# Row normalization by the sum of absolute values: three buffers of 15 rows with the sums split over two engines, in place of four buffers of 13, 13, 13 and 12 rows

## The chip, the core and the metric

The kernel runs on one core of one Trainium2 chip. The metric is the device time of one execution in microseconds (us), the median of three runs. The other cores are idle. The data lies in the device's HBM, and the kernel brings it through the core's on-chip memory, whose 128 partitions are written `P`. It uses two compute engines, VectorE (DVE in the profile) and ScalarE (ACT), and two queues of transfers: the loads are issued by SyncE (SP), the stores by ScalarE.

## What is computed

```python
def setup_inputs():
    batch, seq, dim = 32, 512, 1024
    return {"x": np.random.randn(batch, seq, dim).astype(np.float32)}

def reference(x):
    sums = np.sum(np.abs(x), axis=-1, keepdims=True)
    return (x / (sums + 1e-8)).astype(np.float32)
```

There are 32 x 512 = 16384 rows of 1024 floats (4096 bytes). Each row is divided by the sum of its absolute values. Every element is read once and written once: 67.11 MB in, 67.11 MB out. Spread over 128 partitions, the work is 128 rows for each partition. In this text a "row" is such a row of all partitions together: 128 x 4096 bytes = 0.524 MB to load and as much to store.

## The kernel before

The 128 rows are cut into ten tiles of 13, 13, 13, 12, 13, 13, 13, 12, 13 and 13 rows. Four buffers, of 13, 13, 13 and 12 rows, are used in turn, so tile 4 takes the buffer of tile 0, and its load has to wait until the store of tile 0 has left that buffer.

```python
    R = 13
    SLOTS = [R, R, R, R - 1]
    # ... (cut: the list of the tiles' row counts)

    def piece(flat, i):
        a, k = P * sum(rows[:i]), rows[i]
        return flat[a : a + P * k, :].rearrange("(p r) d -> p r d", p=P)
```

A tile is one contiguous piece of HBM, and each partition gets a contiguous run of it: 13 rows are 13 x 4096 = 53248 bytes. Work on a tile of `k` rows, with `kv = k // 2`:

```python
        nc.vector.tensor_reduce(              # line 50: all k row sums, on VectorE
            out=s[:, :k], in_=x_tile[:, r0 : r0 + k, :],
            axis=mybir.AxisListType.X, op=mybir.AluOpType.add,
            apply_absolute_value=True,
        )
        nc.vector.tensor_scalar_add(out=s[:, :k], in0=s[:, :k], scalar1=EPS)    # line 57
        inv = stats.tile([P, R], FP32)
        nc.vector.reciprocal(out=inv[:, :k], in_=s[:, :k])                      # line 59
        nc.vector.tensor_mul(                 # line 60: scales the first kv rows in place
            out=x_tile[:, r0 : r0 + kv, :], in0=x_tile[:, r0 : r0 + kv, :],
            in1=inv[:, :kv].unsqueeze(2).to_broadcast([P, kv, d]),
        )
        for r in range(kv, k):                # line 67: ScalarE scales the others, row by row
            row = x_tile[:, r0 + r, :]
            nc.scalar.activation(out=row, in_=row,
                func=mybir.ActivationFunctionType.Copy, scale=inv[:, r : r + 1])
```

The loop over the tiles; each engine works through its own instructions in this order, and the engines wait for each other only where data asks for it:

```python
        for i, k in enumerate(rows):
            x_tile = slots[i % len(SLOTS)].tile([P, SLOTS[i % len(SLOTS)], d], FP32)
            nc.sync.dma_start(out=x_tile[:, :k, :], in_=piece(x_flat, i))       # line 77
            normalize(x_tile, 0, k, k // 2)
            nc.scalar.dma_start(out=piece(out_flat, i), in_=x_tile[:, :k, :])   # line 79
```

Of the kernel before, what the change touches and what calls it, by code (L numbers as in the profile page):

```python
# [1 line left out]

# [4 lines left out]

FP32 = mybir.dt.float32
EPS = 1e-8


@with_exitstack
def kernel(
    ctx: ExitStack,
    tc: tile.TileContext,
    x: bass.AP,
    out: bass.AP,
):
    nc = tc.nc
    P = nc.NUM_PARTITIONS  # L20

    x_flat = x.flatten_outer_dims()
    out_flat = out.flatten_outer_dims()
    n, d = x_flat.shape

    R = 13
    SLOTS = [R, R, R, R - 1]
    assert n % P == 0  # L30
    left = n // P
    rows = []
    while left:
        rows.append(min(left, SLOTS[len(rows) % len(SLOTS)]))
        left -= rows[-1]

    def piece(flat, i):
        a, k = P * sum(rows[:i]), rows[i]
        return flat[a : a + P * k, :].rearrange("(p r) d -> p r d", p=P)

    slots = [
        ctx.enter_context(tc.tile_pool(name=f"slot{b}", bufs=1))
        for b in range(len(SLOTS))
    ]
    stats = ctx.enter_context(tc.tile_pool(name="stats", bufs=4))

    def normalize(x_tile, r0, k, kv):

        s = stats.tile([P, R], FP32)
        nc.vector.tensor_reduce(  # L50
            out=s[:, :k],
            in_=x_tile[:, r0 : r0 + k, :],
            axis=mybir.AxisListType.X,
            op=mybir.AluOpType.add,
            apply_absolute_value=True,
        )
        nc.vector.tensor_scalar_add(out=s[:, :k], in0=s[:, :k], scalar1=EPS)  # L57
        inv = stats.tile([P, R], FP32)
        nc.vector.reciprocal(out=inv[:, :k], in_=s[:, :k])  # L59
        nc.vector.tensor_mul(  # L60
            out=x_tile[:, r0 : r0 + kv, :],
            in0=x_tile[:, r0 : r0 + kv, :],
            in1=inv[:, :kv].unsqueeze(2).to_broadcast([P, kv, d]),
        )
        for r in range(kv, k):
            row = x_tile[:, r0 + r, :]
            nc.scalar.activation(  # L67
                out=row,
                in_=row,
                func=mybir.ActivationFunctionType.Copy,  # L70
                scale=inv[:, r : r + 1],
            )

    with tc.manual_schedule():
        for i, k in enumerate(rows):
            x_tile = slots[i % len(SLOTS)].tile([P, SLOTS[i % len(SLOTS)], d], FP32)
            nc.sync.dma_start(out=x_tile[:, :k, :], in_=piece(x_flat, i))  # L77
            normalize(x_tile, 0, k, k // 2)
            nc.scalar.dma_start(out=piece(out_flat, i), in_=x_tile[:, :k, :])


# [1 line left out]
_INS = ['x']  # L83
_OUTS = [((32, 512, 1024), 'float32')]


# [23 lines left out]
```

## Time and profile before

| what | value |
|---|---|
| time, median of three runs | 317.93 us (317.73 to 318.16) |
| span of the profiled execution | 316.0 us |
| VectorE busy | 207.6 us, 66% of the span |
| ScalarE busy | 73.0 us, 23% of the span |
| bytes moved | 134.23 MB, mean 425 GB/s over the span |
| loads, 13 rows, from issue to landing (median) | 42.6 us |
| stores, 13 rows, from issue to landing (median) | 51.3 us |

A profile page describes one execution. It gives the busy time of each engine, then cuts the span into 40 slices of equal length (here 7.9 us) and shows for each, as a digit in tenths, how busy the engine was (9 is 90% or more). The row "DMA" does the same for the core's 16 transfer engines together, and the row "GB/s" says what they moved. "Landing" of a transfer is the moment at which those who wait for it learn that it is complete; "issue" is the moment at which the issuing engine hands it to its queue. The chain of waits starts from the last instruction and goes back, at each step, to what released it.

### The profile page before, as it was taken

How to read it: one execution, taken by the hardware profiler on the slowest of the kernel's cores; microseconds unless marked ns; L12 is line 12 of the kernel's file. 1: busy time of each engine (PE TensorE's matmuls, PEld its weight loads, DVE VectorE, ACT ScalarE, POOL GpSimd, SP SyncE). 2: the span in 40 equal slices, each digit the busy share in tenths (PEclk: the TensorE clock that was granted, in tenths of full speed). 3: DMA queues.
4: the chain of work that ended last, by engine and by line, in shares of the span. 5: the costliest groups of instructions: out<-in, count | busy, mean ns of one | idle time of the engine just before them, and what ended most of it. 6: DMA issues, size and time to landing. Idle time of an engine off the chain costs nothing.

```text
span 316.0 us, 219 instructions
## 1 busy us (share of the span) xinstructions
DVE 207.6 (66%) x40; ACT 73.0 (23%) x69; POOL 0.2 (0%) x4
## 2 busy tenths in 40 slices
DVE  0059999999479707980898099719941995299400
ACT  0010620803500700090009001800430036004500
POOL 0000000000000000000000000000000000000000
DMA  8999999999999999999999999999999999999995
GB/s 324 431 431 431 431 404 431 417 427 427 435 438 438 445 452 431 431 437 409 421 427 438 431 453 452 419 423 431 431 431 431 431 445 428 468 419 431 438 431 236
DMA packets 2881, 134.23 MB, mean 425 GB/s; under 512 B 320, under 2 KB 320, under 8 KB 320
## 3 DMA queue, kind: packets, MB, share of 16 engines
q1 hardware_dynamic: 1440, 67.11, 49.7%
q10 hardware_dynamic: 1440, 67.11, 49.0%
q14 instruction: 1, 0.01, 0.0%
HBM read 67.11 MB, written 67.11 MB: 425 GB/s over the span
## 4 chain that ended last, share of the span: by engine, by line
DVE 33%; DMA 33%; another core or an unknown queue 21%; ACT 6%; issue 0%; SPq 0%; DVEq 0%
DMA x_tile<-in_x_dram 33%; DVE s L50 26%; ACT x_tile L67 6%; DVE x_tile L60 6%; DVE inv L59 0%; DVE s L57 0%; SPq L77 0%; DVEq L59 0%
## 5 line engine op out<-in xcount | busy, mean ns | idle before, releaser
L50 DVE TENSOR_REDUCE s<-x_tile 128x13 f32<-128x13312 f32 (+1 forms) x10 | 138.1, 13806 | 86.6 <-DMA x_tile<-in_x_dram 86.6
L67 ACT ACTIVATE x_tile<-x_tile,inv 128x1024 f32<-128x1024 f32 x68 | 71.8, 1135 | 204.0 <-DVE inv L59 204.0
L60 DVE TENSOR_TENSOR x_tile<-x_tile,inv 128x6144 f32<-128x6144 f32 x10 | 65.6, 6558 | 0.3
L67 ACT ACT_TABLE_LOAD x1 | 1.3, 1283 | 19.5 <-DMA x_tile<-in_x_dram 19.5
L59 DVE RECIPROCAL inv<-s 128x13 f32<-128x13 f32 (+1 forms) x10 | 2.4, 238 | 0.8
L57 DVE TENSOR_SCALAR s<-s 128x13 f32<-128x13 f32 (+1 forms) x10 | 1.7, 174 | 0.3
L94 POOL MEMSET const-bfloat16-1.0<- 128x1 bf16 x1 | 0.1, 102 | 0.0
L94 POOL MEMSET const-uint8-127<- 128x1 uint8 x1 | 0.1, 102 | 0.0
L94 POOL MEMSET const-float32-0.0<- 128x1 f32 x1 | 0.1, 99 | 0.2 <-issue 0.2
L94 POOL MEMSET const-float32-1.0<- 128x1 f32 x1 | 0.1, 99 | 0.0
## 6 DMA issues: line engine op xcount, KB each, us to landing
x_tile<-in_x_dram SPq DMA_DIRECT2D x8, 6656.0 KB, 42.6
out_dram<-x_tile ACTq DMA_DIRECT2D x8, 6656.0 KB, 51.3
x_tile<-in_x_dram SPq DMA_DIRECT2D x2, 6144.0 KB, 64.3
out_dram<-x_tile ACTq DMA_DIRECT2D x2, 6144.0 KB, 56.2
```

Of the source, the lines that this page charges most:

```text
L50: nc.vector.tensor_reduce(out=s[:, :k], in_=x_tile[:, r0 : r0 + k, :], axis=mybir.AxisListType.X, op=mybir.AluOpType.add, apply_absolute_v ...
L57: nc.vector.tensor_scalar_add(out=s[:, :k], in0=s[:, :k], scalar1=EPS)
L59: nc.vector.reciprocal(out=inv[:, :k], in_=s[:, :k])
L60: nc.vector.tensor_mul(out=x_tile[:, r0 : r0 + kv, :], in0=x_tile[:, r0 : r0 + kv, :], in1=inv[:, :kv].unsqueeze(2).to_broadcast([P, kv, d]),)
L67: nc.scalar.activation(out=row, in_=row, func=mybir.ActivationFunctionType.Copy, scale=inv[:, r : r + 1],)
L94: nc = _bacc.Bacc("TRN2", target_bir_lowering=False, num_devices=1)
```

## The change

The changed kernel uses three buffers of 15 rows, and nine tiles: eight of 15 rows and a last one of 8. The summing, which was VectorE's alone, is divided: VectorE sums the first 3/5 of a tile's rows (9 of 15, 4 of 8), ScalarE the others (6 of 15, 4 of 8), one instruction for a row, which writes the absolute values to a row that nobody reads and puts their sum into a column of `s`. The scaling is divided as before, half and half: VectorE takes 7 of 15 rows, ScalarE 8 (4 and 4 in the last tile). The adding of EPS and the reciprocal stay on VectorE; they need the sums of both engines. The aim is to shorten the time between a tile's landing and its store, and to have fewer and larger transfers. The three buffers and the additional row take 3 x 61440 + 4096 = 188416 bytes of each partition, where the four took 51 x 4096 = 208896.

```diff
-    R = 13
-    SLOTS = [R, R, R, R - 1]
+    R = 15
+    BUFS = 3
+    per_partition = n // P
     assert n % P == 0
-    left = n // P
-    rows = []
-    while left:
-        rows.append(min(left, SLOTS[len(rows) % len(SLOTS)]))
-        left -= rows[-1]
+    rows = [R] * (per_partition // R)
+    if per_partition % R:
+        rows.append(per_partition % R)
 ...
-    slots = [
-        ctx.enter_context(tc.tile_pool(name=f"slot{b}", bufs=1))
-        for b in range(len(SLOTS))
-    ]
+    sbuf = ctx.enter_context(tc.tile_pool(name="sbuf", bufs=BUFS))
     stats = ctx.enter_context(tc.tile_pool(name="stats", bufs=4))
+    scratch = ctx.enter_context(tc.tile_pool(name="scratch", bufs=1))
+    junk = scratch.tile([P, d], FP32)
 
-    def normalize(x_tile, r0, k, kv):
+    def normalize(x_tile, k):
 
+        kv = k * 3 // 5
+        km = k // 2
         s = stats.tile([P, R], FP32)
         nc.vector.tensor_reduce(
-            out=s[:, :k],
-            in_=x_tile[:, r0 : r0 + k, :],
+            out=s[:, :kv],
+            in_=x_tile[:, :kv, :],
             axis=mybir.AxisListType.X,
             op=mybir.AluOpType.add,
             apply_absolute_value=True,
         )
+        for r in range(kv, k):
+            nc.scalar.activation(
+                out=junk[:, :],
+                in_=x_tile[:, r, :],
+                func=mybir.ActivationFunctionType.Abs,
+                accum_out=s[:, r : r + 1],
+            )
         nc.vector.tensor_scalar_add(out=s[:, :k], in0=s[:, :k], scalar1=EPS)
 ... (cut: the reciprocal, as before; the scaling, with km in place of kv)
-            x_tile = slots[i % len(SLOTS)].tile([P, SLOTS[i % len(SLOTS)], d], FP32)
+            x_tile = sbuf.tile([P, R, d], FP32)
             nc.sync.dma_start(out=x_tile[:, :k, :], in_=piece(x_flat, i))
-            normalize(x_tile, 0, k, k // 2)
+            normalize(x_tile, k)
             nc.scalar.dma_start(out=piece(out_flat, i), in_=x_tile[:, :k, :])
```

More of the change, by code (lines that the diff above doesn't have):

```diff
@@ L60, in normalize @@
         nc.vector.tensor_mul(
-            out=x_tile[:, r0 : r0 + kv, :],
-            in0=x_tile[:, r0 : r0 + kv, :],
-            in1=inv[:, :kv].unsqueeze(2).to_broadcast([P, kv, d]),
-        )
-        for r in range(kv, k):
-            row = x_tile[:, r0 + r, :]
+            out=x_tile[:, :km, :],
+            in0=x_tile[:, :km, :],
+            in1=inv[:, :km].unsqueeze(2).to_broadcast([P, km, d]),
+        )
+        for r in range(km, k):
+            row = x_tile[:, r, :]
             nc.scalar.activation(
```

## The prediction, made before the changed kernel ran

> **What bounds the kernel now.** I read the slices first, because a kernel that only reads, scales and writes is either limited by the transfers or by a gap in them:
>
> ```profile
> DVE  0059999999479707980898099719941995299400
> ACT  0010620803500700090009001800430036004500
> POOL 0000000000000000000000000000000000000000
> DMA  8999999999999999999999999999999999999995
> GB/s 324 431 431 431 431 404 431 417 427 427 435 438 438 445 452 431 431 437 409 421 427 438 431 453 452 419 423 431 431 431 431 431 445 428 468 419 431 438 431 236
> ```
>
> The DMA row is full from the second slice to the last but one, and it stays full where the rows of both engines show zeros. The GB/s row scatters about 431 because bytes are credited by packets, and 431 is also what stands there when only loads are in flight (slices 2 to 5). So the transfers are the bound, all along, and VectorE at 66% and ScalarE at 23% are not.
>
> The sum confirms it. 256 row transfers of 0.5243 MB (128 in, 128 out) are 134.22 MB; at 431.4 GB/s a row takes **1.215 us** and all of them 311.1 us. Of the 316.0 us of the span that leaves 4.9 us for both ends. I looked at both. The first load is the first long piece of the chain of waits, and the last store can be timed from the end:
>
> ```profile
> 0.73 18.68 DMA x_tile<-in_x_dram
> ...
> DMA to landing us min/median/max: 18.4/53.9/61.3
> ```
>
> The first line has start and length: 13 rows alone would take 15.8 us, so 2.9 us are latency, before the first byte and after the last one together. The second is of the stores: its minimum, 18.4 us, is the last store, which had the transfer engines to itself (15.8 + 2.6). In stretches of 2 us at the end, the DMA share is about 1.00 until 312 us and 0.19 in the stretch to 314: no hole before the end, and after it only completion. Nothing in between can be won without moving fewer bytes.
>
> Is that full row kept up with ease or only just? That is the question for the change, since it takes one buffer away. The waits of the issuing queue answer it:
>
> ```profile
> SPq L77 <- DMA out_dram<-x_tile: 210.0, 6, 57.9
> ...
> x_tile<-in_x_dram SPq DMA_DIRECT2D x8, 6656.0 KB, 42.6
> out_dram<-x_tile ACTq DMA_DIRECT2D x8, 6656.0 KB, 51.3
> ```
>
> The first line (engine, line, waited for: us in total, times, longest) says that the loads from tile 4 on wait for a store to free their buffer. The other two give the median from issue to landing, 42.6 and 51.3 us. With the bandwidth shared by a load and a store, 13 rows take 2 x 13 x 1.215 = 31.6 us plus 2.9 = 34.5. The rest, 8.1 us of a load and 16.8 of a store, is time spent queued behind an earlier transfer: while it lasts, no queue is empty. The kernel before has reserve.
>
> The reserve can also be computed. One turn of the four buffers moves 51 rows in and out: 102 x 1.215 = 123.9 us. A buffer of 13 rows needs 34.5 (load) + 22.0 (the timeline shows tile 9's sum beginning at 274.52 and its store issued at 296.54) + 34.5 (store) = 91.0. Reserve 33 us. Check on one buffer: the load issued at 108.57 landed at 151.28 (8.2 us queued), and the slowest store took 61.3 us (26.8 queued): 35. The method holds.
>
> **What the Trainium skill says.** "DMA: Bandwidth & Descriptors", section Specifications, gives 435 GB/s as the ceiling of the fabric for the 16 engines of a core; the trace agrees, with 431 in its undisturbed slices. The same page, section Queues, rings and completion order, says that each transfer engine takes turns between queues a whole packet at a time. The page counts 2881 packets, of which 320 are tiny; 134.22 MB over the other 2560 is 52.4 KB each, about one partition's run of 13 rows (53.2 KB). So two queues share by packet size, a point for the last tile. "SBUF — State Buffer", section SBUF: two separate sides, says engine accesses and DMA accesses cannot conflict; the trace agrees, since slice 2 with VectorE idle and slice 4 with it at 9 both show 431. "ScalarE: Activation LUTs", section What ACT_TABLE_LOAD costs, gives 186 ns + 0.833 ns per element, and 93 ns more for a per-partition operand: 1132 ns for 1024 elements with a scale operand. The trace has a median of 1132.
>
> **The change part by part.** The bytes stay the same, so the 311.1 us stay. What can move is whether the transfers stay gapless.
>
> *Summing on two engines.* The costs come from these groups:
>
> ```profile
> L50 DVE TENSOR_REDUCE s<-x_tile 128x13 f32<-128x13312 f32 (+1 forms) x10 | 138.1, 13806 | 86.6 <-DMA x_tile<-in_x_dram 86.6
> L67 ACT ACTIVATE x_tile<-x_tile,inv 128x1024 f32<-128x1024 f32 x68 | 71.8, 1135 | 204.0 <-DVE inv L59 204.0
> L60 DVE TENSOR_TENSOR x_tile<-x_tile,inv 128x6144 f32<-128x6144 f32 x10 | 65.6, 6558 | 0.3
> ```
>
> The sum costs 138.1 / 128 = 1.079 us a row, VectorE's scaling 6558 / 6 = 1.093 us a row, ScalarE's scaling 7.38 us for seven rows and 6.35 for six, so about 1.04 a further row. For 15 rows: VectorE sums 9 rows, 9.7 us; beside it ScalarE sums 6. Nothing in this trace is such an instruction; from the page's formula I estimate 1.04 to 1.13 us and add 0.2 for handing out the sum, 1.3 us, so 7.8 us, hidden behind VectorE. Then EPS and reciprocal, 0.5 us with the gaps (33.46 to 33.97 before). Then VectorE scales 7 rows, 7.7 us, beside ScalarE's 8 rows, 8.4 us. Landing to store: 9.7 + 0.5 + 8.4 = **18.7 us for 15 rows**, against 22.0 for 13. VectorE falls to 76 x 1.079 + 60 x 1.093 + about 4 = 151 us; ScalarE rises to 68 x 1.06 + 52 x 1.3 + 1.3 = 141 us. None of that is on the bound.
>
> *Three buffers of 15.* A turn moves 45 rows in and out: 90 x 1.215 = 109.4 us. A buffer needs 2 x 15 x 1.215 + 2.9 = 39.4 (load) + 18.7 + 39.4 (store) = 97.5. **Reserve 12 us**, down from 33 but positive: the transfers stay gapless. With the old division of work, 15 rows would need some 16.2 + 0.5 + 8.4 = 25.1 us and leave 5.5; so the shorter computing pays for part of the missing buffer and earns nothing by itself.
>
> *The start.* Load 0 (18.2 us alone) lands at about 21.8, its store is issued near 41. The loads alone have 45 rows, 54.7 us, to move. No hole. When store 0 begins near 42, 33 rows are loaded; the last 12 of load 2 share with it (24 x 1.215 = 29 us) and end near 71. Store 0's last 3 rows end near 75, and load 3, which waits for that, begins near 78. In between the store queue works alone, with store 1 issued near 61 behind store 0.
>
> *The end.* The last load has 8 rows and shares with a 15-row store. By packet size it gets 8/23 of the rate, so it needs 23 rows' time, 28 us. It starts when load 7 ends: 120 rows in, and tiles 0 to 5 (90 rows) and a little more out, 212 x 1.215 + 2 = 260 us; it lands near 290. Its computing: sum max(4.3, 4 x 1.3 = 5.2) + 0.5 + 4.3 = 10 us; the store is issued near 300. By then all but 8 rows must have been moved for the queue to run dry: 248 rows x 1.215 from 2.0 us ends at 303. So the last store is in time, **by about 3 us less the latency of its first byte, 1 to 2 us**. That is narrow; it was narrow before as well (issued 296.54, with 243 rows moved at 297).
>
> Sum: 311.1 us of transfers, the same ends of 4.9 us, no hole, or one of up to 1 us at the end. The runs before lie 1.9 us above the profiled span. I expect 318.1 us.
>
> **The rivals.** *The shorter computing pays.* If the chain of waits is read by its shares, VectorE's sums hold 26% of it, 82 us, and six of fifteen rows leave VectorE: that would promise up to 33 us. Against it: the chain passes through the sums only because each buffer must be filled and emptied; the DMA row is full meanwhile. Time would be some 285 us, under the 311 that the bytes need. I give it almost nothing.
> *Three buffers are too few.* If computing were 12 us longer than I think, or shares unequal for long, both queues would run dry once a tile; each microsecond missing in a turn costs 1/3 us a tile, 3 us over nine tiles. For it: the loads already wait for stores today. Against it: 33 us of reserve, and its check on one buffer. Time would be 321 to 327.
> *The tail hole.* If the last load lands 3 us later than computed, or a ScalarE sum costs 2 us, the last store comes late and its 8 rows (9.7 us) stand behind a hole of 2 to 4 us: 320 to 322.
> *The runs of 61440 bytes move at another rate.* Nothing in the trace speaks for it: the 12-row transfers keep the rate of the 13-row ones. One per cent of rate would be 3 us either way.
>
> **Range and chances.** The bytes forbid more than about 2 us of gain; a missing microsecond at either end gives 316.8. Upward the tail hole and a small loss of rate set 320.6. Slower by 2% means 324.3, which only too few buffers or a rate 2% lower would do: 0.06. Faster by 2% means 311.6, the bare bytes: 0.01. The rest is within 2%.
>
> **What would show it.** Right: DMA digits of 9 from the second slice to the last but one; medians of 42 us for 15-row loads and 47 for stores (39.4 each, and the reserve of some 10 to 12 us divided between them); VectorE near 151 and ScalarE near 141 us; nine tiles, landing to store 18.7 us. Wrong: digits of 7 or 8 once in each turn (too few buffers), a low slice only before the last (tail hole), digits of 9 with a GB/s row that is lower throughout (rate). What I rely on most is that one queue alone fills all 16 engines while the other is empty.

## The result and the profile after

The changed kernel took 319.45 us (319.08 to 319.98, four runs) against 318.01: a ratio of 1.0047, with a 95% interval of 1.003 to 1.0065. It is slower by about 1.5 us, well within 2% and clear of the scatter. The forecast was 318.1 us with a range of 316.8 to 320.6.

The slices of the page after, in the same form as before (7.95 us each):

```profile
DVE  0029999207950019910596009920498008940910
ACT  1026997307560017820557008630459007550910
POOL 0000000000000000000000000000000000000000
DMA  9999999999999999999999999999999999999985
GB/s 363 394 479 394 471 355 417 448 418 448 425 440 433 433 433 433 448 417 456 409 456 409 463 409 456 402 463 409 456 402 463 402 463 391 447 414 465 394 370 227
```

The DMA row is as full as before through all turns of the three buffers. The first difference is at the end: an 8 in the last slice but one, and 394, 370 and 227 GB/s in the last three. (The saw teeth in the GB/s row are larger packets being credited whole; neighbours average the same 431.) So the loss has to be looked for in the last 20 us. Here is that end in stretches of 2 us; the columns are stretch, length, busy time of VectorE, ScalarE and GpSimd with the number of their instructions, clock, DMA share, GB/s. (A stretch is credited with the packets that start in it, so its share can exceed 1, and a hole shows up to a packet's length, about 2 us, early.)

```profile
300.00:302.00 2.00, 2.00 (x1) 2.00 (x3) 0.00 (x0) 1.00 1.13 492
302.00:304.00 2.00, 1.68 (x1) 1.52 (x2) 0.00 (x0) 1.00 0.43 184
304.00:306.00 2.00, 0.00 (x0) 0.00 (x0) 0.00 (x0) 1.00 1.06 453
306.00:308.00 2.00, 0.00 (x0) 0.00 (x0) 0.00 (x0) 1.00 0.72 311
...
312.00:314.00 2.00, 0.00 (x0) 0.00 (x0) 0.00 (x0) 1.00 0.87 377
314.00:316.00 2.00, 0.00 (x0) 0.00 (x0) 0.00 (x0) 1.00 0.27 115
```

The transfers thin out between 302 and 304 us while VectorE and ScalarE still work on the last tile, and they end raggedly: averaged over the sixteen engines, 1.9 us of idle time lie after 312 us, against 1.1 at the end of the kernel before. Why the hole is there is seen in the timeline of the changed kernel (start, length, engine, line, instruction, idle time before it):

```profile
282.85 0.34 ACTq L85 DMA_DIRECT2D out_dram<-x_tile  x1
294.09 4.42 DVE L49 TENSOR_REDUCE s<-x_tile 128x4 f32<-128x4096 f32 x1 [12.07 <-DMA x_tile<-in_x_dram]
303.76 0.34 ACTq L85 DMA_DIRECT2D out_dram<-x_tile  x1
```

The list of its transfers has the median time from issue to landing in the last column:

```profile
x_tile<-in_x_dram SPq DMA_DIRECT2D x8, 7680.0 KB, 42.4
out_dram<-x_tile ACTq DMA_DIRECT2D x8, 7680.0 KB, 47.6
x_tile<-in_x_dram SPq DMA_DIRECT2D x1, 4096.0 KB, 36.6
out_dram<-x_tile ACTq DMA_DIRECT2D x1, 4096.0 KB, 13.5
```

The last tile's load landed at 294.09 us, not near 290, and its store was issued at 303.76, when the earlier stores were running out: the sixteen engines completed the store of tile 7 between 303.3 and 307.6 us. The last store took 13.5 us instead of the 12.3 of an undisturbed one (9.7 + 2.6). The medians of 42.4 and 47.6 us are the ones computed (42 and 47): the turns run as forecast.

The trace records every packet and, for each transfer, sixteen completions, one from each transfer engine. Summed and divided by 16, the packets took 312.75 us against 312.31 before, and between the first and the last packet the engines were idle for 3.09 us on average against 1.40. That is 0.44 + 1.69 us of the 2.2 us by which the two profiled spans differ. The idle time lies after 300 us, 2.7 us of it: 0.9 in the hole at 302 to 306 us and the rest in the ragged end. And the sixteen completions explain the late landing: those of the last load came between 285.1 and 294.1 us, **8.9 us apart**. In the kernel before the sixteen are never more than 1.8 us apart, less than the 1.97 us that one packet takes. A tile is usable when the slowest of the sixteen is done.

What the engines paid was close to the estimate. The groups, as before:

```profile
L49 DVE TENSOR_REDUCE s<-x_tile 128x9 f32<-128x9216 f32 (+1 forms) x9 | 82.5, 9162 | 150.3 <-DMA x_tile<-in_x_dram 150.1
L57 ACT ACTIVATE junk<-x_tile 128x1024 f32<-128x1024 f32 x52 | 54.9, 1057 | 144.3 <-DMA x_tile<-in_x_dram 142.5
L73 ACT ACTIVATE x_tile<-x_tile,inv 128x1024 f32<-128x1024 f32 x68 | 71.7, 1136 | 25.8 <-DVE inv L65 25.8
L57 ACT ACTIVATION_READ_ACCUMULATOR junk<-x_tile 128x1 f32 x52 | 9.7, 186 | 0.0
```

A sum on ScalarE is two instructions, 1057 and 186 ns, that follow each other at 1.18 us a row. VectorE is busy for 151.7 us (151 expected), ScalarE for 132.7 (141 expected).

### The profile page after: what moved, and what is told of

Read it like the earlier page. It is cut to its first block, busy times and chain, and to the rows that moved or that the text cites. A ratio compares the mean times of both kernels' runs of the same rounds, so it can differ in the third digit from the quotient of the medians.

```text
span 318.2 us, 315 instructions
## 1 busy us (share of the span) xinstructions
DVE 151.7 (48%) x36; ACT 132.7 (42%) x173; POOL 0.2 (0%) x4
## 4 chain that ended last, share of the span: by engine, by line
DMA 52%; another core or an unknown queue 26%; DVE 8%; ACT 8%; issue 1%; SPq 0%; ACTq 0%; DVEq 0%
DMA x_tile<-in_x_dram 37%; DMA out_dram<-x_tile 15%; DVE s L49 6%; ACT x_tile L73 5%; ACT junk L57 3%; DVE x_tile L66 1%; SPq L83 0%; DVE inv L65 0%; DVE s L63 0%; ACTq L85 0%; DVEq L63 0%
## 5 line engine op out<-in xcount | busy, mean ns | idle before, releaser
L49 DVE TENSOR_REDUCE s<-x_tile 128x9 f32<-128x9216 f32 (+1 forms) x9 | 82.5, 9162 | 150.3 <-DMA x_tile<-in_x_dram 150.1
L57 ACT ACTIVATE junk<-x_tile 128x1024 f32<-128x1024 f32 x52 | 54.9, 1057 | 144.3 <-DMA x_tile<-in_x_dram 142.5
L66 DVE TENSOR_TENSOR x_tile<-x_tile,inv 128x7168 f32<-128x7168 f32 (+1 forms) x9 | 65.4, 7270 | 0.3
L57 ACT ACTIVATION_READ_ACCUMULATOR junk<-x_tile 128x1 f32 x52 | 9.7, 186 | 0.0
L65 DVE RECIPROCAL inv<-s 128x15 f32<-128x15 f32 (+1 forms) x9 | 2.2, 245 | 0.3
L63 DVE TENSOR_SCALAR s<-s 128x15 f32<-128x15 f32 (+1 forms) x9 | 1.6, 174 | 1.2 <-ACT junk L57 0.3
## 6 DMA issues: line engine op xcount, KB each, us to landing
x_tile<-in_x_dram SPq DMA_DIRECT2D x8, 7680.0 KB, 42.4
out_dram<-x_tile ACTq DMA_DIRECT2D x8, 7680.0 KB, 47.6
x_tile<-in_x_dram SPq DMA_DIRECT2D x1, 4096.0 KB, 36.6
out_dram<-x_tile ACTq DMA_DIRECT2D x1, 4096.0 KB, 13.5
```

The source lines that it names most:

```text
L49: nc.vector.tensor_reduce(out=s[:, :kv], in_=x_tile[:, :kv, :], axis=mybir.AxisListType.X, op=mybir.AluOpType.add, apply_absolute_value=True,)
L57: nc.scalar.activation(out=junk[:, :], in_=x_tile[:, r, :], func=mybir.ActivationFunctionType.Abs, accum_out=s[:, r : r + 1],)
L66: nc.vector.tensor_mul(out=x_tile[:, :km, :], in0=x_tile[:, :km, :], in1=inv[:, :km].unsqueeze(2).to_broadcast([P, km, d]),)
```

## The experiments

Three theories stood against each other. **T**: the loss is made at the end, by how late the last load lands, plus its computing, against how long the earlier stores keep the queue busy. **R**: three buffers lose a little in every turn (from one use of a buffer to the next). **P**: packets of 61440 bytes are slower. P has the trace against it at once: the median packet of 61440 bytes took 2267 ns, that of 53248 bytes 1966 ns, 27.1 bytes a nanosecond both. The runs below are compared with the kernel before on the same chip, where it took 318.45 (first four runs), 317.95 (the pair, the small tile first, and the longest of the longer computings) and 317.94 us (the others).

**The last tile in two halves.** The changed kernel with

```diff
-            normalize(x_tile, k)
-            nc.scalar.dma_start(out=piece(out_flat, i), in_=x_tile[:, :k, :])
+            parts = [(0, 4), (4, 8)] if i == 8 else [(0, k)]
+            for lo, hi in parts:
+                normalize(x_tile[:, lo:hi, :], hi - lo)
+                nc.scalar.dma_start(out=piece(out_flat, i)[:, lo:hi, :], in_=x_tile[:, lo:hi, :])
```

> The changed kernel (319.45 us), with the last tile of 8 rows summed, scaled and stored in two halves of 4 rows, so that the first store is issued some 4 to 5 us earlier, near 299 us instead of 303.8, before the store of tile 7 has left the queue. Theory T (the loss is made at the very end: the last load lands late because its 16 shares drift apart, and the last store finds an empty queue): the hole at 303 to 305 us closes, time falls by 1 to 1.5 us, to 318.0 to 318.5. Theory R (three buffers lose a little in every turn) and theory P (packets of 61440 bytes are slower): no change, 319.2 to 319.7.

Measured: 319.83 us, ratio 1.0039 (1.0025 to 1.0053). Not cured. Its stretches of 2 us say why: the hole was no longer before the last store, it had moved ahead of the store of tile 7:

```profile
284.00:286.00 2.00, 2.00 (x1) 2.00 (x3) 0.00 (x0) 1.00 0.50 213
286.00:288.00 2.00, 0.74 (x1) 1.54 (x2) 0.00 (x0) 1.00 0.19 82
288.00:290.00 2.00, 0.00 (x0) 0.00 (x0) 0.00 (x0) 1.00 1.19 508
```

In this execution the load of tile 7 was complete at 268.8 us (264.0 in the first profile of the changed kernel, by instructions that are the same up to there), with its completions 6.6 us apart; its store was issued at 287.6, after the store of tile 6 had ended (282.9 to 286.9). This execution was the longest of the thirteen (320.71 us); where the others had their hole was not recorded. So the place of the hole can differ from execution to execution; what both profiles show is that the sixteen engines are apart and the store queue is short. T as I had put it, one hole in one place, was too narrow.

**Dividing the sums alone.** The kernel before, four buffers and ten tiles, with

```diff
+        ks = k * 3 // 5
-            out=s[:, :k],
-            in_=x_tile[:, r0 : r0 + k, :],
+            out=s[:, :ks],
+            in_=x_tile[:, r0 : r0 + ks, :],
 ...
+        for r in range(ks, k):
+            nc.scalar.activation(
+                out=junk[:, :], in_=x_tile[:, r0 + r, :],
+                func=mybir.ActivationFunctionType.Abs, accum_out=s[:, r : r + 1],
+            )
```

> The kernel before, its four buffers and ten tiles unchanged, but with the sums divided as in the changed kernel (3/5 of the rows on VectorE, the others on ScalarE; the row that nobody reads is kept in bfloat16, as there is no room for a float32 one). Landing to store falls from 22.0 to some 17 us. All theories: the transfers are full already, so 317.7 to 318.3, the same as before. If dividing the sums had a price or a gain of its own, it would show here alone.

Measured: 320.38 us (317.77 to 320.76, nineteen runs), ratio 1.0044 (1.003 to 1.0059). All theories missed: shorter computing by itself made the four-buffer kernel slower. Its end in the timeline:

```profile
283.68 7.62 DVE L53 TENSOR_REDUCE s<-x_tile 128x7 f32<-128x7168 f32 x1 [16.53 <-DMA x_tile<-in_x_dram]
...
299.30 0.34 ACTq L89 DMA_DIRECT2D out_dram<-x_tile  x1
```

The last load landed at 283.7 us, where it had landed at 274.5. The computing after it is 6.4 us shorter (15.6 instead of 22.0), but the store was still issued 2.8 us later than before (299.3 and 296.5). Part of the delay is drift, as the sixteen completions of this load were 5.4 us apart; their mean came 5.9 us later than in the kernel before (279.2 and 273.3). The reason suggests itself: the total rate is fixed, so a first store that is issued 6 us earlier (34.9 us, 41.4 before) takes its share from the loads from then on. A tile that is stored earlier is a load that is finished later. The pair after the next two runs tests it.

**The transfers alone.** The changed kernel without its computing; the output is x, nothing is summed or scaled.

```diff
-            normalize(x_tile, k)
```

> The changed kernel's transfers alone: three buffers of 15 rows, nine tiles, load and store, with all sums and scaling left out (the output is x). Reserve of a turn grows from 12 to about 30 us and the last store is issued when its load lands. T: no hole in the turns nor at the end, 317.5 to 318.5. R: the same. P: the loss stays, 319.2 to 319.8.

Measured: 319.85 us (318.32 to 320.95), ratio 1.0031 (1.001 to 1.0051). The median was P's; three of the twelve executions lie within T's figures, and the profiled one was the longest. In it the packets are at the same rate, but the completions of the last load lay 14 us apart (292.5 to 306.5 us), and from 304 to 307 us only a few engines had work. With no computing at all the stores start at 21.9 us and the loads end only shortly before the end of everything, so the slowest engine's lag goes into the time undiminished. I had expected that no computing means no hole; the end depends on when the last load lands as well, not on the computing alone.

**Three buffers with VectorE's sums.** The changed kernel with `kv = k` and ScalarE's sums taken out:

```diff
-        kv = k * 3 // 5
+        kv = k
 ...
-        for r in range(kv, k):
-            nc.scalar.activation(out=junk[:, :], in_=x_tile[:, r, :],
-                func=mybir.ActivationFunctionType.Abs, accum_out=s[:, r : r + 1])
```

> The changed kernel with three buffers of 15 and nine tiles, but VectorE sums all rows as before (25.1 us from landing to store for 15 rows, 13.4 for the last 8, where the changed kernel has 18.7 and 9.6). Reserve of a turn 5.5 us instead of 12. T: the last store is issued about 3.5 us later, 307, and the hole grows by as much: 322 to 323.5, with DMA digits of 9 until 300 us. R: holes in every turn too, digits of 8 in the middle, over 324. P: 319.5.

Measured: 321.2 us (320.12 to 321.73), ratio 1.0077 (1.0047 to 1.0107); a little under T's figure. The engines were idle for 4.0 us between 280 and 290 us, waiting for the store of tile 7 and not, as T had it, for the last one, and hardly at all in the turns. So with three buffers the divided sums seem to help, where with four they hurt; it is not clear of noise, as the changed kernel's ratio was 1.0047 (1.003 to 1.0065).

**Dividing the sums in the last tile only, and in the first four only.** These two are a pair: the first keeps the start as it was and shortens the end, the second the other way round. Against the four-buffer kernel with divided sums:

```diff
-        ks = k * 3 // 5
+        ks = k * 3 // 5 if i == 9 else k     # first kernel of the pair
+        ks = k * 3 // 5 if i < 4 else k      # second kernel of the pair
```

> The kernel before with its four buffers and VectorE's sums, but in the last tile alone the sums are divided (8 of 13 rows on VectorE). Theory T (the loss lies in the end: how late the last load lands, plus its computing, against how long the earlier stores keep the queue busy): the last load lands near 274.5 as before, its store is issued near 290 instead of 296.5, well before the store of tile 8 has ended, and no run has a hole: 317.6 to 318.2, at or a little under the kernel before on the same chip, with less scatter. Theory S (dividing the sums costs something of its own, by the load on ScalarE or its queue): the same as before, 318 to 319, since only one tile is divided.

> The opposite: the sums are divided in the first four tiles alone, the other six are summed by VectorE. T: the first stores start 5 us earlier, take their share of the bandwidth from then on, and the last load lands 6 to 9 us later than in the kernel before, near 281 to 284 us; with 22 us of computing its store is issued near 303 to 306, after the store of tile 8 has ended near 299: a hole of 5 to 8 us, 323 to 326 us. S: four tiles of ten are divided, so less than half of the loss of the kernel divided throughout (320.4 against 318.4): 318.5 to 319.5.

Measured: 318.02 us for the first, ratio 1.0001 (0.9992 to 1.001), and 326.19 us for the second, ratio 1.0253 (1.0235 to 1.027). The first fits both theories; the second is near T's figures and far from S's. The second one's end in the timeline:

```profile
279.55 14.02 DVE L53 TENSOR_REDUCE s<-x_tile 128x13 f32<-128x13312 f32 x1 [9.28 <-DMA x_tile<-in_x_dram]
301.57 0.34 ACTq L89 DMA_DIRECT2D out_dram<-x_tile  x1
```

And in stretches of 2 us:

```profile
296.00:298.00 2.00, 2.00 (x1) 2.00 (x3) 0.00 (x0) 1.00 0.19 80
298.00:300.00 2.00, 2.00 (x1) 2.00 (x3) 0.00 (x0) 1.00 0.00 0
300.00:302.00 2.00, 0.71 (x1) 1.54 (x2) 0.00 (x0) 1.00 0.00 0
```

Four shortened tiles at the beginning put the last load back from 274.5 to 279.6 us, and with the old 22.0 us of computing behind it the transfer engines stood still for 5 us. (The profiled execution took 321.88 us and was the quickest of five; the other four took 325.9 to 326.4. In the profiled one the completions of a transfer were only about 1 us apart, so this delay is not drift; what the other four lost in addition was not seen.) The first kernel of the pair issues its last store at 289.8 us, 9 us before the store ahead of it has ended, has no hole, and is no faster than the kernel before: that kernel is already at the floor of 256 rows and two ends.

**The small tile first.** The changed kernel with

```diff
-        rows.append(per_partition % R)
+        rows.insert(0, per_partition % R)
```

> The changed kernel with its tile of 8 rows first and the eight tiles of 15 rows after it; nothing else differs. T: the last tile is now one of 15 rows, its load gets an equal share and lands near 282 to 284, its computing takes 18.7 us, and its store is issued near 302, while the store before it ends near 296: a hole of some 6 us, 323 to 326. R (a loss in every turn of three buffers) and P (packet size): the same turns and packets, 319.2 to 320.2.

The four executions scattered from 323.2 to 336.1 us, so no ratio is given; the quickest, the only one that can be set against the other kernels with so much scatter, lies within T's figures, and each was slower than every run of the kernel before and of the changed kernel. The profiled one (328.5 us) has T's hole, and larger than expected, in the slices with the digits 0 and 5:

```profile
DMA  8999999899898998989989899898998999980597
GB/s 321 433 481 365 433 486 433 361 474 466 384 475 369 474 459 384 474 369 474 466 376 474 376 466 474 369 481 384 459 466 376 466 399 444 474 384 24 241 414 308
```

The last load of 15 rows landed at 287.5 us with its completions 8.5 us apart; its store was issued at 306.3. Even in the quickest execution the order of the nine tiles, with the same turns and the same packets, costs 3.5 us or more, over twice what the whole change did.

**Longer computing on purpose.** The changed kernel with additional sums in tiles 0 to 6, whose results are not used:

```diff
+        for _ in range(1 if i < 7 else 0):     # 2 in the third kernel
+            again = stats.tile([P, R], FP32)
+            nc.vector.tensor_reduce(out=again[:, :9], in_=x_tile[:, :9, :], ...)   # 13 rows in the second
```

> The changed kernel with VectorE's sum of 9 rows done twice in tiles 0 to 6, 9.75 us more from landing to store, VectorE still under 80% busy. The computed reserve of a turn is 12 us, so nearly all of it is used. T with the reserve calculation: no holes of the turns after the first; a hole of up to 3 us near 78 us, where load 3 waits for the first store, and the end about 2 us later: 320 to 323. R (three buffers have no reserve): two turns and more at 9.75 us, 335 or over.

> The same with a second sum of 13 rows, 14 us more from landing to store in tiles 0 to 6, with VectorE at about 32 us of the 36.5 us that a tile's transfers take, so that it is not itself the bound. The computed reserve of 12 us is exceeded by 2 us in each turn: the first hole of about 3 us near 78 us, small holes in each later turn, 6 to 8 us in all: 322 to 327. If the reserve is larger than computed (queues drifting apart fill the holes), as with 9.75 us more: 320 to 323. If it is smaller by the drift of some 4 us: over 328.

> The changed kernel with VectorE's sum of 9 rows done three times instead of once in tiles 0 to 6 (the two additional results are not used), 19.5 us more from landing to store: the computed reserve of 12 us is exceeded by 7.7. T and the reserve calculation: from the third tile on each turn of three tiles is 7.7 us too long, holes in the middle of the span, DMA digits of 7 or 8, about 20 to 25 us in all: 338 to 345 us. A rival by which three buffers have no reserve at all (R): 19.5 us a turn, over two turns some 40 us and more, 360.

Measured: 325.68 us with 9.75 us more (1.0227, 1.0202 to 1.0251), 340.82 with 14 us more (1.071, 1.0691 to 1.0729) and 343.24 with 19.5 us more (1.0791, 1.0774 to 1.0808). The last hit its forecast for a wrong reason and is no test of the reserve: VectorE then needs 3 x 9.75 + 7.6 + 0.6 = 37.5 us for a tile, more than the 36.5 us of its transfers, and its row on the page is full:

```profile
DVE  0049999999999999999999999999999999908200
```

The first two are tests, and both took longer than the forecasts that go with a reserve of 12 us: the first by 2.7 us, the second by almost 14 (its forecast has "over 328" for a reserve that is smaller by the drift). The DMA rows of the two pages (slices of 8.1 and 8.5 us):

```profile
DMA  9999899996999998999989899999999999999993
DMA  8999998988999889999999979998899999999994
```

With 9.75 us more, the 6 in the first row is the hole before load 3: the engines were idle for 2.0 us near 75, as forecast. From 90 to 312 us they were idle for less than 0.2 us, so no turn had a hole, as the reserve of 12 us says. But little of it was left: from a load to the next load into the same buffer 110.2 to 111.1 us passed, where gapless transfers need 109.4. Most of the rest of the loss lies in packets that took longer than their size asks for, 6.2 us of excess for each engine against 2.8 in the changed kernel, in groups near 80 and near 195 us. With 14 us more, the holes were 2.1 us near 75 and 7.3 us between 90 and 320, a little over the 6 to 8 in all that were forecast; the other 12 us lost are again packets that took too long (14.7 us of excess), and completions lay up to 13 us apart. So by its holes the reserve lies between 9.75 and 14 us, and the calculation left out something else that costs time once the reserve is nearly used. R is out: three buffers do have a reserve, and the changed kernel stays within it.

**The late stores cut in two.** The changed kernel once more for comparison, and then with

```diff
+            if i in (6, 7):
+                h = 8
+                nc.scalar.dma_start(out=piece(out_flat, i)[:, :h, :], in_=x_tile[:, :h, :])
+                nc.scalar.dma_start(out=piece(out_flat, i)[:, h:, :], in_=x_tile[:, h:k, :])
```

> The changed kernel once more, for a second profile of it and as the measure for the next run on the same chip. T: 319 to 320.5, and in the profile the last transfers again drift apart: the sixteen completions of the last load lie more than 4 us apart (1.8 us in the kernel before), with a hole before the last or the last but one store. R and P: the same time, but the sixteen completions as close as in the kernel before, and the loss spread over the span.

> The changed kernel, but the stores of tiles 6 and 7 are two transfers each, of 8 and 7 rows, so their packets are half as large (32768 and 28672 bytes). If two queues share by packet size, the last load (packets of 32768 bytes) gets half the rate instead of a third, and the load of tile 7 two thirds: the last load lands near 280 to 284 us instead of 294, and the last store is issued near 290 to 294. T: the hole before the last store closes: 318 to 319; what is left of the loss lies before the store of tile 7. If packet size has no part in the sharing: the last load lands near 290 to 294 as before and the time stays at 319 to 320.5.

Measured: the changed kernel again 319.73 us (1.0054, 1.0036 to 1.0071); with the cut stores **318.39 us (1.001, 1.0002 to 1.0018)**. Three quarters of the loss are gone, with three buffers of 15, nine tiles and divided sums all in place. In the second profile of the changed kernel the last load's completions were 6.3 us apart; this time there was no hole before the last store (issued at 301.4, while the store of tile 7 was completed from 303.6 on), but the completions of the last store were 3.9 us apart. All of its late idle time, 2.9 us, lies in the ragged end, and the time is the same: the loss needs no hole before a store. With the cut stores, the timeline:

```profile
280.82 4.42 DVE L49 TENSOR_REDUCE s<-x_tile 128x4 f32<-128x4096 f32 x1 [1.54 <-DMA x_tile<-in_x_dram]
290.50 0.34 ACTq L90 DMA_DIRECT2D out_dram<-x_tile  x1
```

The time from issue to landing of its last load, and the same stretches of 2 us as above:

```profile
x_tile<-in_x_dram SPq DMA_DIRECT2D x1, 4096.0 KB, 23.1
```

```profile
300.00:302.00 2.00, 0.00 (x0) 0.00 (x0) 0.00 (x0) 1.00 1.00 430
302.00:304.00 2.00, 0.00 (x0) 0.00 (x0) 0.00 (x0) 1.00 1.06 457
304.00:306.00 2.00, 0.00 (x0) 0.00 (x0) 0.00 (x0) 1.00 0.95 408
```

The last load landed at 280.8 instead of 294.1 us, after 23.1 us instead of 36.6, because half-size packets of the stores beside it leave it a larger share, and its completions were 1.2 us apart. The hole is gone, and so is the ragged end: the completions of the last store were 1.8 us apart, and 1.3 us of idle time are left at the end (1.1 in the kernel before). Which of the two, the earlier landing or the smaller drift, saved how much, this run does not separate.

## Why the prediction was right, and where it was not

- **The bound.** Right. All kernels here that keep the transfers full take 318 us, whatever the engines do. The 33 us that the chain's shares seemed to promise did not exist.
- **The reserve of three buffers.** The sign was right: no turn of the changed kernel has a hole. The size holds only roughly: with 9.75 of the 12 us used up the turns still had no hole, but they were already 1 to 2 us too long, and the run lost 6 us. Two terms are missing from the sum, and no run separates them. One is the drift of the sixteen engines (4.1 to 4.6 us for the stores in the changed kernel's turns), since a load waits for the slowest engine of a store and the computing for the slowest engine of a load. The other is the latency, which I took from transfers that ran alone: load 3 of the changed kernel, issued to its empty queue while the stores were running, began its first packet 4.0 us later, load 0 after 1.0 us.
- **The divided sums.** The durations were right: 1.18 us a row against an estimate of 1.3, 18.8 us from landing to store (264.04 to 282.85 in tile 7) against 18.7. That the shorter computing "earns nothing by itself" was too kind for four buffers, where alone it cost 0.44%: the last load landed 9 us later, some 5 to 6 of them by the earlier stores (5.0 in the kernel with four shortened tiles, which hardly drifted), the others by drift. I had read the time from landing to store as something that can only gain by being shortened.
- **The end.** This is the step that carried the result, and the rival called the tail hole is the one that came true. The last load was put near 290 us by its share of 8/23; it landed at 294.1. The share was about right: the mean of its sixteen completions is 287.8 us, and with the cut stores, where packet size gives it half the rate, it landed 19.5 us after the load before it, against 19.4 computed for 16 rows. What failed is that I took one moment for sixteen engines. The last store was to be issued at 300 us, 3 us before the earlier ones had left the queue; it was issued 3.8 us later, when some engines had already run dry. The hole cost 0.9 us, within "one of up to 1 us", but the ragged end, which the prediction did not have, brought the loss to about 1.5 us. That the time stayed in the range is owed to the room the range left for this rival, not to the calculation of the end.
- **Rate by packet size.** Right: 27.1 bytes a nanosecond at both sizes.

What stays open is why the engines drift further apart in some kernels and executions than in others. In the kernel before they stayed within 1.8 us for the whole span, in two executions of the changed kernel the completions of a store were about 4 us apart from the second store on, and in the run with the last tile in halves 7 us, by the same instructions. The spread is there soon after the first store joins the loads; in the copy it grew from 3 to 14 us, for the stores of the run with the last tile in halves it shrank from 7 to 4. No experiment here set it.

## What to carry to other kernels

When the transfers are full from end to end, the only thing left to lose is the end: compare the moment when the last load will land, plus its computing, with the moment when the earlier stores will have left the queue, and keep several microseconds between them, for a transfer is done when the slowest engine is done. Shortening the computing everywhere can make that worse, because stores that begin earlier hold back the loads; where the end is what costs time, shorten it in the last tile, or give the last load a larger share by making the packets beside it smaller. Judge a buffer count by the reserve of one turn, and leave several microseconds of it unused.

## What the runs showed of the hardware

- The sixteen completions of one transfer can lie far apart: at most 1.8 us in the kernel before, up to 4.6 us in the turns of the changed one and 8.9 us in its last load, 14 us in the last load of the copy. The median time to landing does not show it.
- Two queues share by packet size: the same load of 8 rows took 36.6 us beside packets of 61440 bytes and 23.1 us beside packets of about half of that. Without the time behind the load before it these are 30.1 and 19.5 us; 23 and 16 rows at 1.215 us, the shares by packet size, come to 27.9 and 19.4, and the longer one has the drift in it.
- A transfer issued to an empty queue begins later when the other queue is at work. From issue to first packet it was 1.0 us for load 3 of the kernel with 14 us more computing, when no store was running, and 4.0 us for load 3 of the changed kernel beside the stores; the first store of the changed kernel, beside the loads, took 5.8 us.
- Packets seem to take longer when a queue starts again after it ran dry. Per engine, the packets took 312.3 us in the kernel before and 324.7 in the kernel with 14 us more computing, for the same bytes; packets that took clearly longer than their size asks for were 38 and 327, and they came in groups at the start, at the first store, and near the holes. It was not tested by itself.
